# A two-block transformer kernel: x parked in DRAM around two feed-forwards, their first two jobs begun in another order, the gate's product on VectorE

## The chip, the cores and the metric

One core of one Trainium2 chip runs the whole program. The metric is the device time of one execution in microseconds (us), and of several executions the median. TensorE (PE) multiplies 128x128 blocks, VectorE (DVE), ScalarE (ACT) and GpSimd (POOL) do elementwise work, and SyncE (SP) issues most of the loads. Each engine works through its own queue in order.

## The reference

Two transformer blocks run one behind the other on 512 tokens of width 1024. All matmuls are float32. What matters here are their two feed-forwards, each on a normed x that came out of a residual addition just before:

```python
def rmsnorm(x, g):
    y = x32 * lax.rsqrt(jnp.mean(jnp.square(x32), axis=-1, keepdims=True) + EPS)
    return (y * g).astype(x.dtype)

# first block, its end
x = x + jnp.einsum('bsd,de->bse', merged, w_out[l])
h2 = rmsnorm(x, norm_mlp_g[l])
up = jnp.square(jax.nn.relu(jnp.einsum('bsd,df->bsf', h2, w_up[l])))      # 1024 -> 4096
x = x + jnp.einsum('bsf,fd->bsd', up, w_down[l])

# second block, its end
x = x + cross_attention(rms_norm(x, xattn_norm_g[l]), ...)
x = x + swiglu(rms_norm(x, ffn_norm_g[l]), w_ffn_gate[l], w_ffn_up[l], w_ffn_down[l])
return rms_norm(x, final_norm_g)

def swiglu(xn, w_gate, w_up, w_down):                                     # 1024 -> 2816
    return (jax.nn.silu(xn @ w_gate) * (xn @ w_up)) @ w_down
```

The rest (attention of three kinds, a recurrence, convolutions, gates) stands in the same program and is not touched.

## The kernel before

x lies transposed: eight tiles `x` of 128 features by 512 tokens. A float32 operand is held as two parts, hi and lo (`split_to`, L267: ACT casts hi, DVE subtracts to get lo), and a product takes three matmuls (`mm3`, L168). Every matmul is recorded on L159, so the trace tells them apart by their tiles.

**The up projections of both feed-forwards are made by a scheme with seven half-size products instead of eight.** `norm_sums` (L316) turns each pair of x tiles (one even, one odd) into operands: `ae` and `ao` (ACT, x times the gain), the sums `f1` and `f2` (DVE, L336 to L339), and then hi and lo of s1 (half of `ae`), f1, f2 and `ao`. There are four pairs. s1 needs the even tile of its pair alone; f1, f2 and `ao` need the odd one too. `weight_sums` (L347) does the same for a pair of weight slabs: raw loads on SP, casts on ACT, seven DVE operations. `halves` (L382) is one job: it makes two output tiles `ca` and `cb` out of two weight slabs by the products 1, 5, 2, 6, 7, 4, 3 (`product`, L375: twelve 128x256 matmuls each, three for each pair of x tiles). The products 1, 6, 7, 4 add up in one PSUM bank `u`, and a copy by ACT takes the bank's state after each of them (L397 to `ca`, L404 and L407 to `cb`, L411 to `ca`), so the product behind a copy waits for it. Product 5 and 3 go to `v`, product 2 to `p2`. DVE finishes with L400, L408 and L413 and hands the two tiles to `out`.

The norm's factor is not in the operands. `square` (L452) collects the squares of x on ACT and POOL (L459, L469). `rstd_tok` (L463) sums them over the features with eight small matmuls on `ones`, works out 1/sqrt on DVE (L479, then L282 to L286, thirteen small operations) and makes two diagonal tiles `dgh` and `dgl` (L491, L492). `rstd_row` (L498) spreads them over the partitions with two matmuls and a copy (L507) into `row`. Each `out` multiplies by `row` first.

**The start of a feed-forward.** The residual projection before it (`residual_stage`, L658, or `residual_keep`, L1492) takes m = 0 to 7: product into PSUM, DVE adds x (L668, L1499), then `norm_sums`. In `residual_stage` x is read back from DRAM by a POOL transfer (L666); in `residual_keep` it is in SBUF already. The first two jobs of the feed-forward start before the last pair of x is ready, with `lead=True`: they first do pairs 0 to 2 of the products 1, 5, 2, yield, then do pair 3 of them and L397 and L400, yield, then product 6 and L404, and so on. `halves_lead` (L416) lays the two jobs out in turn:

```python
for _ in range(2):
    for g in jobs:
        next(g)
r = self.rstd_tok(self.sq)
for g in jobs:
    next(g)
self.r, self.row = self.rstd_row(r)
self.sq = None
self.rounds(jobs)
```

So the norm stands between L400 and product 6 of both jobs, and `row` between products 6 and 7.

**The feed-forwards.** `ffn1` (L1011) has eight groups of two jobs; its `out` squares a relu on DVE and splits into `uh`, `ul`. `ffn2` (L1503) has five groups; jobs alternate between the gate's weights (`out_g`: times row L1525, ACT's tanh L1527, L1528, giving `tg`) and the other's (`out_u`: times row L1534, then the product of gate and up on POOL, L1535, then the split into `fah` and `fal`, L273 and L274). The down projections of a group (`downs`, L1017 and L1507) are filled in between the jobs of the next (`fill`, L438): each is twelve 128x512 matmuls into a bank and an addition into `x[m]` (L1025, L1515). x stays in SBUF all the while. `finish` (L1553) makes the last down projection and the last norm.

**What sets the order.** The text gives an order, and a planner that runs when the program is built decides each engine's queue from it: the earliest instruction of the text that it believes ready comes first, so instructions of an engine can pass each other. All elementwise tiles of 128x512 come from one pool of 56 slots (`T`, L116), and the planner hands them out in the order in which the text first writes them: of the 1186 tiles of that pool in the instruction list of the kernel before, none comes out of that order. A tile's first writer thus never stands ahead of the first writer of an earlier tile in the planner's time. The PSUM banks are eight.

Of the kernel before, what the change touches and what calls it, by code (L numbers as in the profile page):

```python
# [9 lines left out]
F32 = mybir.dt.float32  # L10
# [4 lines left out]
P = 128  # L15
S = 512
D = 1024
KT = 8
# [76 lines left out]
class Net:  # L95
# [217 lines left out]

    def norm_sums(self, x, g, kt, sq, st):  # L316


        nc = self.nc
        H = S // 2  # L320
        if kt % 2 == 0:
            a = self.T("ae")
            nc.scalar.activation(a, x, AF.Copy, scale=self.col(g, kt))
            self.square(x, sq)
            st["even"] = a
            return
        e, o = st.pop("even"), self.T("ao")
        nc.scalar.activation(o, x, AF.Copy, scale=self.col(g, kt))
        self.square(x, sq)
        kp = kt // 2  # L330
        if kp % 2 == 0:
            st["one"] = (self.R("s1h"), self.R("s1l"))
        c = (kp % 2) * H
        s1 = tuple(t[:, c : c + H] for t in st["one"])
        f1, f2 = self.T("f1"), self.T("f2")
        nc.vector.tensor_sub(f1[:, :H], e[:, H:], o[:, H:])  # L336
        nc.vector.tensor_sub(f1[:, H:], f1[:, :H], e[:, :H])
        nc.vector.tensor_sub(f2[:, :H], e[:, :H], e[:, H:])
        nc.vector.tensor_add(f2[:, H:], o[:, :H], f1[:, H:])  # L339
        self.split_to(s1[0], s1[1], e[:, :H])  # L340
        p1, p2, po = self.split(f1, s="f1"), self.split(f2, s="f2"), self.split(o, s="ao")
        cut = lambda p, i: tuple(t[:, i * H : i * H + H] for t in p)
        st.setdefault("S", []).append(
            {1: s1, 2: cut(po, 0), 4: cut(po, 1), 5: cut(p1, 0), 6: cut(p1, 1), 7: cut(p2, 0), 3: cut(p2, 1)}
        )
# [36 lines left out]
    def halves(self, wname, j, st, out, lead=False):  # L382

        nc = self.nc
        H = S // 2
        w = self.weight_sums(wname, j)
        u, v, p2 = self.PS("u"), self.PS("v"), self.PS("p2")
        if lead:
            ks = (range(KT // 2 - 1), range(KT // 2 - 1, KT // 2))
            for i, ps in ((1, u), (5, v), (2, p2)):  # L390
                self.product(ps, st, w, i, True, ks[0])
            yield
        else:
            ks = (None, range(KT // 2))
        a, b = self.T("ca"), self.T("cb")
        self.product(u, st, w, 1, True, ks[1])
        nc.scalar.copy(a[:, :H], u[:, :H])  # L397
        self.product(v, st, w, 5, True, ks[1])
        self.product(p2, st, w, 2, True, ks[1])
        nc.vector.tensor_add(a[:, :H], p2[:, :H], a[:, :H])  # L400
        if lead:
            yield
        self.product(u, st, w, 6, False)
        nc.scalar.copy(b[:, :H], u[:, :H])  # L404
        yield
        self.product(u, st, w, 7, False)
        nc.scalar.copy(b[:, H:], u[:, :H])  # L407
        nc.vector.tensor_sub(b[:, H:], v[:, :H], b[:, H:])  # L408
        yield
        self.product(u, st, w, 4, False)  # L410
        nc.scalar.copy(a[:, H:], u[:, :H])  # L411
        self.product(v, st, w, 3, False)
        nc.vector.tensor_sub(b[:, :H], v[:, :H], b[:, :H])  # L413
        out(a, b)

    def halves_lead(self, jobs):  # L416

        nc = self.nc
        for _ in range(2):
            for g in jobs:  # L420
                next(g)
        r = self.rstd_tok(self.sq)
        for g in jobs:
            next(g)
        self.r, self.row = self.rstd_row(r)
        self.sq = None
        self.rounds(jobs)

    def rounds(self, jobs):
        jobs = list(jobs)  # L430
# [227 lines left out]
    def residual_stage(self, wname, act, g, reload, halves=False):  # L658

        nc = self.nc  # L660
        sq = []
        new, nact, st = [], [], {}
        pss = self.proj_T_lead([(wname, 0), (wname, 1)], act)
        for m in range(8):
            x = self.T("x")
            nc.gpsimd.dma_start(out=x, in_=reload[m])  # L666
            ps = pss[m] if m < 2 else run(self.proj_T(wname, m, act))
            nc.vector.tensor_add(x, ps, x)  # L668
            new.append(x)
            if halves:  # L670
                self.norm_sums(x, g, m, sq, st)
            else:
                nact.append(self.norm_tile(x, g, m, sq))
        self.x, self.act, self.sq = new, st if halves else nact, sq

    def consts1(self):
        nc = self.nc
# [333 lines left out]
    def ffn1(self, g_next):  # L1011
        nc = self.nc
        st = self.act
        sq = []
        nact = []

        def downs(g, u):  # L1017
            ws = {}

            def down(m):  # L1020
                if m % 2 == 0:
                    ws[0] = self.slab("w_down", g * 4 + m // 2)
                ps = self.PS()
                self.acc_T(ps, ws[0], (m % 2) * S, u, 0, 4, True, True)
                nc.vector.tensor_add(self.x[m], ps, self.x[m])  # L1025
                if g == 7:
                    nact.append(self.norm_tile(self.x[m], g_next, m, sq))

            return [lambda m=m: down(m) for m in range(8)]

        prev = []
        for g in range(8):
            cur = []

            def out(*tiles):
                for t in tiles:
                    nc.vector.tensor_mul(t, t, self.row)
                    nc.vector.scalar_tensor_tensor(out=t, in0=t, scalar=0.0, in1=t, op0=ALU.max, op1=ALU.mult)
                    cur.append(self.split(t, s="u"))

            jobs = [self.halves("w_up", 2 * g + i, st, out, g == 0) for i in range(2)]
            if g == 0:
                self.halves_lead(jobs)
            else:
                self.fill(jobs[0], prev[:4], (1, 2))
                self.fill(jobs[1], prev[4:], (1, 2))
            prev = downs(g, cur)
        for f in prev:
            f()
        self.act, self.sq = nact, sq  # L1050
# [441 lines left out]
    def residual_keep(self, wname, act, g):  # L1492
        nc = self.nc
        sq = []
        st = {}
        pss = self.proj_T_lead([(wname, 0), (wname, 1)], act)
        for m in range(8):
            ps = pss[m] if m < 2 else run(self.proj_T(wname, m, act))
            nc.vector.tensor_add(self.x[m], ps, self.x[m])  # L1499
            self.norm_sums(self.x[m], g, m, sq, st)  # L1500
        self.act, self.sq = st, sq

    def ffn2(self):  # L1503
        nc = self.nc
        st = self.act

        def downs(g, u):  # L1507
            ws = {}

            def down(m):  # L1510
                if m % 2 == 0:
                    ws[0] = self.slab("w_fd", g * 4 + m // 2)
                ps = self.PS()
                self.acc_T(ps, ws[0], (m % 2) * S, u, 0, 4, True, True)
                nc.vector.tensor_add(self.x[m], ps, self.x[m])  # L1515

            return [lambda m=m: down(m) for m in range(8)]

        prev, gate = [], []
        for g, pairs in enumerate(((0, 1), (2, 3), (4, 5), (6, 7), (8, 9, 10))):  # L1520
            cur = []

            def out_g(*tiles):
                for z in tiles:
                    nc.vector.tensor_mul(z, z, self.row)  # L1525
                    t = self.T("tg")
                    nc.scalar.activation(t, z, AF.Tanh, scale=0.5)  # L1527
                    nc.vector.scalar_tensor_tensor(out=t, in0=t, scalar=1.0, in1=z, op0=ALU.add, op1=ALU.mult)  # L1528
                    gate.append(t)

            def out_u(*tiles):
                for z in tiles:
                    t = gate.pop(0)
                    nc.vector.tensor_mul(z, z, self.row)  # L1534
                    nc.gpsimd.tensor_mul(t, t, z)  # L1535
                    cur.append(self.split(t, 0.5, s="fa"))

            jobs = [
                self.halves(w, j, st, o, g == 0 and j == 0) for j in pairs for w, o in (("w_fg", out_g), ("w_fu", out_u))
            ]  # L1540
            if g == 0:
                self.halves_lead(jobs[:2])
                self.rounds(jobs[2:])
            else:
                n = len(prev)
                for i, job in enumerate(jobs):
                    fs = prev[i * n // len(jobs) : (i + 1) * n // len(jobs)]
                    self.fill(job, fs, (1, 1))
            prev = downs(g, cur) if g < 4 else cur
# [202 lines left out]
```

## Time and profile before

| | |
|---|---|
| median of 3 runs | 1959.29 us (1958.47 to 1959.96) |
| the profiled execution, its own time | 1957.96 us |
| its span, first to last instruction | 1956.2 us |
| granted clock of TensorE, mean | 0.982 |
| PE busy, share of the span | 1873.5 us, 96% |
| DVE busy | 1375.9 us, 70% |
| ACT, POOL busy | 868.8 us, 295.2 us |

The profile is of one execution, so its rows are added up against its own time, 1957.96 us, which is 1.33 us under the median of the runs. Busy time of PE is not PE at its peak: the clock granted to it can be half, and matmuls are then twice as long. In the rows below "<-" stands between an engine that waited and what ended its wait, or between a tile and what it is made from; names lose their numbers, so `ps` is any bank of that name.

### The profile page before, as it was taken

How to read it: one execution, taken by the hardware profiler on the slowest of the kernel's cores; microseconds unless marked ns; L12 is line 12 of the kernel's file. 1: busy time of each engine (PE TensorE's matmuls, PEld its weight loads, DVE VectorE, ACT ScalarE, POOL GpSimd, SP SyncE). 2: the span in 40 equal slices, each digit the busy share in tenths (PEclk: the TensorE clock that was granted, in tenths of full speed). 3: DMA queues.
4: the chain of work that ended last, by engine and by line, in shares of the span. 5: the costliest groups of instructions: out<-in, count | busy, mean ns of one | idle time of the engine just before them, and what ended most of it. 6: DMA issues, size and time to landing. Idle time of an engine off the chain costs nothing.

```text
span 1956.2 us, 26791 instructions
## 1 busy us (share of the span) xinstructions
PE 1873.5 (96%) x10376; PEld 1609.9 (82%) x10376; DVE 1375.9 (70%) x2548; ACT 868.8 (44%) x1499; POOL 295.2 (15%) x270
## 2 busy tenths in 40 slices
PE   8999999999979999999999999999999979999997
PEld 6787777888869999998977788888988778888886
DVE  7477777687688877867676665465566978778764
ACT  5366655454453333333343444243335544444433
POOL 2322310201210000002022110132100210110112
PEclk9999999999989999999999999999999999999998
DMA  5222322222422333334321222234422223222221
GB/s 178 81 83 92 102 72 79 88 66 65 130 86 88 107 97 98 108 97 139 96 76 65 78 85 76 98 107 135 146 97 80 87 71 108 87 87 98 86 81 60
DMA packets 54383, 183.84 MB, mean 94 GB/s; under 512 B 6528, under 2 KB 9632, under 8 KB 54256
## 3 DMA queue, kind: packets, MB, share of 16 engines
q1 hardware_dynamic: 50016, 170.78, 26.7%
q0 software_dynamic: 3552, 10.82, 1.9%
q8 instruction: 81, 1.33, 0.3%
q10 hardware_dynamic: 688, 0.53, 0.1%
q14 instruction: 46, 0.38, 0.1%
HBM read 177.87 MB, written 4.24 MB: 93 GB/s over the span
## 4 chain that ended last, share of the span: by engine, by line
PE 74%; DVE 15%; ACT 4%; DMA 3%; POOL 2%; issue 2%; DVEq 0%; SPq 0%; POOLq 0%; ACTq 0%
PE ps L159 54%; PE u L159 9%; PE v L159 3%; PE s L159 2%; PE o L159 2%; DVE wl L271 2%; PE p L159 2%; DVE wl L362 1%; DMA raw<-in_w_fg 1%; PE pv L159 1%; POOL tg L1535 1%; PE pt L163 1%; DVE sbl L367 1%; DVE sal L364 1%; DMA raw<-in_w_fu 1%
## 5 line engine op out<-in xcount | busy, mean ns | idle before, releaser
L159 PE MATMUL ps<-xx,wh 128*128 128x512 f32 x1424 | 445.6, 394 | 2.7 <-ACT wh L270 2.7
L270 ACT CAST wh<-raw 128x1024 fp32r<-128x1024 f32 (+4 forms) x252 | 255.0, 1017 | 340.0 <-PE ps L159 228.4
L271 DVE TENSOR_TENSOR wl<-raw,wh 128x1024 fp32r<-128x1024 f32 (+4 forms) x252 | 315.4, 1253 | 87.7 <-ACT wh L270 85.6
L159 PEld LDWEIGHTS ps<-xx,wh 128*128 128x128 f32 x1424 | 261.7, 188 | 59.0 <-ACT wh L270 3.1
L159 PE MATMUL ps<-xx,wl 128*128 128x512 f32 x712 | 278.0, 390 | 1.6 <-DVE wl L271 1.6
L159 PE MATMUL ps<-wh,xx 128*128 128x512 f32 (+1 forms) x512 | 157.1, 379 | 5.7 <-ACT wh L270 5.5
L159 PEld LDWEIGHTS ps<-xx,wl 128*128 128x128 f32 x712 | 133.7, 188 | 31.1 <-DVE wl L271 2.5
L159 PEld LDWEIGHTS ps<-wh,xx 128*128 128x128 f32 x512 | 95.2, 191 | 23.2 <-ACT wh L270 5.5
L459 POOL TENSOR_TENSOR sq<-sq,sq 128x512 f32<-128x512 f32 (+1 forms) x46 | 61.9, 1347 | 258.3 <-ACT sq L457 258.0
L159 PE MATMUL ps<-ul,wh 128*128 128x512 f32 x256 | 100.2, 391 | 0.0
L159 PE MATMUL ps<-uh,wh 128*128 128x512 f32 x256 | 100.0, 391 | 0.0
L159 PE MATMUL ps<-uh,wl 128*128 128x512 f32 x256 | 99.5, 389 | 0.0
L159 PE MATMUL ps<-wl,xx 128*128 128x512 f32 (+1 forms) x256 | 96.7, 378 | 2.1 <-DVE wl L271 2.1
L159 PE MATMUL ps<-fah,wh 128*128 128x512 f32 (+1 forms) x200 | 75.0, 375 | 1.4 <-ACT fah L273 1.4
L159 PE MATMUL ps<-fal,wh 128*128 128x512 f32 (+1 forms) x200 | 74.7, 373 | 0.0
L159 PE MATMUL ps<-fah,wl 128*128 128x512 f32 (+1 forms) x200 | 74.5, 372 | 0.0
L1025 DVE TENSOR_TENSOR x<-ps,x 128x512 f32<-128x512 f32 x64 | 44.1, 689 | 41.0 <-PE ps L159 41.0
L361 ACT CAST sah<-sa 128x1024 fp32r<-128x1024 f32 x38 | 39.9, 1051 | 66.3 <-DVE sa L359 62.2
L159 PE MATMUL u<-f1h,sah 128*128 128x256 f32 x152 | 46.8, 308 | 20.1 <-ACT ca L397 20.1
L1535 POOL TENSOR_TENSOR tg<-tg,ca 128x512 f32<-128x512 f32 x11 | 20.3, 1849 | 298.2 <-DVE ca L1534 298.2
L159 PE MATMUL v<-f2h,wl 128*128 128x256 f32 x304 | 60.9, 283 | 0.0
L999 POOL TENSOR_TENSOR gt<-gt,gt 128x512 f32<-128x512 f32 x24 | 36.0, 1501 | 155.4 <-DVE gt L995 155.4
(451 smaller groups left out, 5050.8 us busy)
## 6 DMA issues: line engine op xcount, KB each, us to landing
raw<-in_w_up SPq DMA_DIRECT2D x32, 512.0 KB, 3.5
raw<-in_w_down SPq DMA_DIRECT2D x32, 512.0 KB, 3.6
raw<-in_w_gate SPq DMA_DIRECT2D x24, 512.0 KB, 3.4
raw<-in_w_qkv SPq DMA_DIRECT2D x23, 512.0 KB, 3.6
raw<-in_w_fg SPq DMA_DIRECT2D x22, 512.0 KB, 3.5
raw<-in_w_fu SPq DMA_DIRECT2D x22, 512.0 KB, 3.4
raw<-in_w_fd SPq DMA_DIRECT2D x16, 512.0 KB, 3.4
raw<-in_w_conv SPq DMA_DIRECT2D x12, 512.0 KB, 3.5
```

What stands on the lines that cost most here:

```text
L159: self.nc.tensor.matmul(out, **k)
L163: self.nc.tensor.transpose(out, a, ident)
L270: nc.scalar.copy(hi, src)
L271: nc.vector.tensor_sub(lo, src, hi.bitcast(F32))
L361: nc.scalar.copy(ha, sa)
L362: nc.vector.tensor_sub(la, ra, h.bitcast(F32))
L364: nc.vector.tensor_sub(da, sa, ha.bitcast(F32))
L367: nc.vector.tensor_sub(db, sb, hb.bitcast(F32))
L459: nc.gpsimd.tensor_add(sq[0][:, sl], sq[0][:, sl], sq[1][:, sl])
L999: nc.gpsimd.tensor_add(merged[m], merged[m], t)
L1025: nc.vector.tensor_add(self.x[m], ps, self.x[m])
L1535: nc.gpsimd.tensor_mul(t, t, z)
```

## The change

1. `residual_stage` and `residual_keep` write each new x tile to a DRAM tile `xs` by a POOL transfer (`put`), and forget the SBUF tile. The first group's down projections in both feed-forwards read it back by a POOL transfer (`get`) between their matmuls and their addition.
2. In the first two jobs of a feed-forward, product 1 is written whole and copied (L397) ahead of products 5 and 2, of which pairs 0 to 2 come first; pair 3 follows after the yield, product 2 ahead of product 5. A third yield stands ahead of `out`. `halves_lead` puts the norm (`rstd_tok`) behind product 6 of both jobs, and `row` behind products 4 and 3 of the first job.
3. The product of gate and up in `out_u` moves from POOL to DVE.

```diff
+    def put(self, m, x):
+        if m == 0:
+            self.xs = self.dp.tile([8, P, S], F32, tag="xs", bufs=1, name=self.name("xs"))
+        self.nc.gpsimd.dma_start(out=self.xs[m], in_=x)
+
+    def get(self, m):
+        x = self.T("x")
+        self.nc.gpsimd.dma_start(out=x, in_=self.xs[m])
+        return x
...
         if lead:
-            ks = (range(KT // 2 - 1), range(KT // 2 - 1, KT // 2))
-            for i, ps in ((1, u), (5, v), (2, p2)):
-                self.product(ps, st, w, i, True, ks[0])
+            late = range(KT // 2 - 1, KT // 2)
+            early = range(KT // 2 - 1)
+        a, b = self.T("ca"), self.T("cb")
+        self.product(u, st, w, 1, True)
+        nc.scalar.copy(a[:, :H], u[:, :H])
+        if lead:
+            self.product(v, st, w, 5, True, early)
+            self.product(p2, st, w, 2, True, early)
             yield
+            self.product(p2, st, w, 2, True, late)
+            self.product(v, st, w, 5, True, late)
         else:
-            ks = (None, range(KT // 2))
-        a, b = self.T("ca"), self.T("cb")
-        self.product(u, st, w, 1, True, ks[1])
-        nc.scalar.copy(a[:, :H], u[:, :H])
-        self.product(v, st, w, 5, True, ks[1])
-        self.product(p2, st, w, 2, True, ks[1])
+            self.product(v, st, w, 5, True)
+            self.product(p2, st, w, 2, True)
         nc.vector.tensor_add(a[:, :H], p2[:, :H], a[:, :H])
         if lead:
             yield
...
         nc.vector.tensor_sub(b[:, :H], v[:, :H], b[:, :H])
+        if lead:
+            yield
         out(a, b)
 
     def halves_lead(self, jobs):
-        nc = self.nc
-        for _ in range(2):
-            for g in jobs:
-                next(g)
+        a, b = jobs
+        for _ in range(3):
+            next(a)
+            next(b)
         r = self.rstd_tok(self.sq)
-        for g in jobs:
+        for g in (a, b, a):
             next(g)
         self.r, self.row = self.rstd_row(r)
         self.sq = None
-        self.rounds(jobs)
+        self.rounds((a, b))
...
             if halves:
+                self.put(m, x)
                 self.norm_sums(x, g, m, sq, st)
...
                 self.acc_T(ps, ws[0], (m % 2) * S, u, 0, 4, True, True)
+                if g == 0:
+                    self.x[m] = self.get(m)
                 nc.vector.tensor_add(self.x[m], ps, self.x[m])
...
                     t = gate.pop(0)
                     nc.vector.tensor_mul(z, z, self.row)
-                    nc.gpsimd.tensor_mul(t, t, z)
+                    nc.vector.tensor_mul(t, t, z)
                     cur.append(self.split(t, 0.5, s="fa"))
```

`put` and `get` stand in the same way in `residual_keep` (behind L1499) and in both `downs` (L1025, L1515).

## Rows read from the trace of the kernel before

**Rows 1.** The page's busy time by engine.

```profile
PE 1873.5 (96%) x10376; PEld 1609.9 (82%) x10376; DVE 1375.9 (70%) x2548; ACT 868.8 (44%) x1499; POOL 295.2 (15%) x270
```

**Rows 2.** Stretches: length, busy PE, PEld, DVE, ACT, POOL, PE clock, DMA share.

```profile
552.00:593.00 41.00, 30.26 (x183) 28.29 (x182) 29.33 (x58) 18.77 (x34) 6.19 (x6) 0.79 0.20 64
593.00:885.00 292.00, 292.00 (x1840) 265.01 (x1839) 225.34 (x320) 111.08 (x165) 0.00 (x0) 1.00 0.33 102
884.00:920.00 36.00, 36.00 (x163) 29.74 (x162) 26.19 (x30) 16.52 (x24) 14.06 (x15) 1.00 0.43 145
1544.00:1584.00 40.00, 29.67 (x184) 28.13 (x183) 29.07 (x58) 17.34 (x29) 6.08 (x2) 0.79 0.15 53
1584.00:1910.00 326.00, 304.18 (x2083) 280.93 (x2081) 252.34 (x346) 136.37 (x217) 41.86 (x22) 0.98 0.27 91
```

**Rows 3.** PE in time, first lead, 569 to 593: start, duration, [idle before].

```profile
569.06 1.87 PE L159 MATMUL ps<-ones,sq 128*128 128x2 f32 x8 [2.48 <-POOL sq L469]
...
578.04 0.28 PE L159 MATMUL u<-f1h,sal 128*128 128x256 f32 x1
581.91 0.51 PE L159 MATMUL ps<-dgh,onesr 128*128 128x512 f32 x1 [3.59 <-DVE dgh L491]
...
582.76 0.28 PE L159 MATMUL u<-f2h,sbh 128*128 128x256 f32 x1
...
587.13 0.28 PE L159 MATMUL u<-aoh,sbh 128*128 128x256 f32 x1
...
592.77 0.28 PE L159 MATMUL v<-f2h,wl 128*128 128x256 f32 x1
```

**Rows 4.** ACT in time, first lead: the first copies to cb.

```profile
581.30 0.64 ACT L404 COPY cb<-u 128x256 f32<-128x256 f32 x2
```

**Rows 5.** DVE in time, first lead: `dgh`, then the first and last of `out`.

```profile
580.46 0.47 DVE L491 TENSOR_SCALAR dgh<-ident,s 128x128 fp32r<-128x128 f32 x2
...
589.17 0.69 DVE L1037 TENSOR_TENSOR ca<-ca,row 128x512 f32<-128x512 f32 x1 [1.01 <-ACT ca L411]
...
599.46 0.69 DVE L271 TENSOR_TENSOR ul<-cb,uh 128x512 fp32r<-128x512 f32 x1
```

**Rows 6.** Two of PE's waits in the second lead, 1544 to 1584: total, times, longest.

```profile
PE u L159 <- ACT cb L404: 3.4, 1, 3.4
PE ps L159 <- DVE dgh L491: 2.7, 1, 2.7
```

**Rows 7.** PE in time, second lead: where product 6 starts and the jobs end.

```profile
1556.28 0.58 PE L159 MATMUL v<-f1l,sah 128*128 128x256 f32 x1 [0.51 <-DVE f1l L271]
...
1561.44 0.56 PE L159 MATMUL u<-f1h,sah 128*128 128x256 f32 x1
...
1583.85 0.28 PE L159 MATMUL v<-f2h,wl 128*128 128x256 f32 x1
```

**Rows 8.** PE's waits in the second feed-forward, 1584 to 1912.

```profile
PE u L159 <- ACT ca L397: 20.1, 12, 2.4
PE ps L159 <- ACT fah L273: 1.4, 1, 1.4
```

**Rows 9.** The gated product on POOL, second tile of a job: ns min/median/max, first and last start.

```profile
L1535 POOL TENSOR_TENSOR tg<-tg,cb x11: 1267/2126/2276, 1589.7 to 1908.0; 128x512 f32<-128x512 f32 x11
```

**Rows 10.** DVE in time, second feed-forward: two subtractions of one size.

```profile
1742.72 1.99 DVE L362 TENSOR_TENSOR wl<-raw,wh 128x1024 fp32r<-128x1024 f32 x1
...
1745.83 1.21 DVE L367 TENSOR_TENSOR sbl<-sb,sbh 128x1024 fp32r<-128x1024 f32 x1
```

**Rows 11.** A 10 us stretch behind one of the longer waits, columns as in rows 2.

```profile
1750.00:1760.00 10.00, 10.00 (x57) 8.93 (x56) 5.53 (x10) 2.41 (x5) 0.00 (x0) 0.83 0.15 52
```

**Rows 12.** Transfers between x and DRAM on POOL, and their time to landing.

```profile
L1067 POOL DMA_DIRECT2D xd<-x x8: 539/557/562, 892.6 to 911.9; - x8
L666 POOL DMA_DIRECT2D x<-xd x8: 536/553/553, 1344.2 to 1378.7; - x8
...
DMA to landing us min/median/max: 2.3/2.8/5.2
```

More of the change, by code (lines that the diff above doesn't have):

```diff
@@ L673, in residual_stage @@
                 nact.append(self.norm_tile(x, g, m, sq))
-        self.x, self.act, self.sq = new, st if halves else nact, sq
+        self.x, self.act, self.sq = [None] * 8 if halves else new, st if halves else nact, sq
     def consts1(self):
@@ L1499, in residual_keep @@
             nc.vector.tensor_add(self.x[m], ps, self.x[m])
+            self.put(m, self.x[m])
             self.norm_sums(self.x[m], g, m, sq, st)
+        self.x = [None] * 8
         self.act, self.sq = st, sq
@@ L1514, in down @@
                 self.acc_T(ps, ws[0], (m % 2) * S, u, 0, 4, True, True)
+                if g == 0:
+                    self.x[m] = self.get(m)
                 nc.vector.tensor_add(self.x[m], ps, self.x[m])
```

## The prediction

> **What bounds the kernel now.** I read the page first. PE is busy for 1873.5 of 1956.2 us [rows 1], so the kernel is a chain of matmuls, and a change that leaves their number alone can win only where PE stands idle or runs at half its clock. Next I read the busy time by stretches. The first feed-forward behind its start keeps PE busy for all of 292 us at full clock: nothing to gain there. Its start (552 to 593) has 30.3 us of work in 41, the second start (1544 to 1584) 29.7 in 40, both at a mean granted clock of 0.79, and the second feed-forward 304.2 in 326 at 0.98 [rows 2]. These three places hold 10.7, 10.3 and 21.8 us of idle time, 42.8 in all, and some time at half clock on top. The change touches just these three. So the question is what ends PE's waits there, and for that I read the waits of PE in each.
>
> In the first start the longest wait is 3.6 us, for `dgh`, the norm's diagonal tile [rows 3]. The reader should see what stands in the way: product 6 of both jobs ends at 578.04, product 7 needs ACT's copies of it to `cb` (L404), and those come at 581.30 [rows 4], just after DVE has begun `dgh` at 580.46 [rows 5]. `cb` is first written behind the norm in the text, and slots go out in the text's order, so the copies were planned behind the norm's DVE chain. In the second start the same two things cost 3.4 us (`cb`) and 2.7 us (`dgh`) [rows 6]. In the second feed-forward nearly all waits are one line: product 6 for `ca` (L397), 20.1 us in 12 waits, and one for `fah`, 1.4 us [rows 8]. `ca` of a job is first written behind `fah` of the job before, and ACT's queue has it behind `fah`, which waits for the product on POOL. That one lasts 1.27 us at its shortest and 2.13 at the median [rows 9]: POOL and DVE hold each other up, and a DVE subtraction of 1.21 us takes 1.99 beside it [rows 10].
>
> **The parts of the change.**
>
> *The norm later.* It removes nothing; it moves the eight `ones` matmuls, the DVE chain, `dgh`, `dgl` and the two `row` matmuls behind product 6, and so puts `cb`'s first write ahead of `dgh`'s. Behind product 6 PE then has products 7, 7, 4 and 3 without the norm. The 48 matmuls of products 4 and 3 start from 587.13 to 592.77 [rows 3], 0.12 us apart, so the four products are 48 x 0.12 = 5.8 us of cover for the norm's chain.
>
> First start: from product 6's end (578.2) to the end of the two jobs (592.9) it is 14.7 us. The 72 matmuls are 72 x 0.12 = 8.6 us, the two `row` matmuls 0.85 (581.91 to 582.76) [rows 3]: 9.5 us. The difference, 5.2 us, is the wait of 3.6 and about 1.5 of half clock behind it (product 7 of both jobs, 24 matmuls, took 582.76 to 587.13, 4.4 us instead of 2.9). Next late is `out`: its DVE chain runs 11 us, 589.17 to 600.1 [rows 5], and the first down projection needs its last piece. It starts as soon as the first job's product 3 is done, 5.8 us behind product 6, at about 584.2, and ends at about 595, 5 us earlier. I take 4.5. Below, -2, if the chain runs later than its cover and PE's queue has `row` ahead of the second job's product 4; above, 5.2 plus the 2.5 us that PE waits for the last square ahead of `ones` [rows 3], 7.7. The `ones` matmuls (1.87 us, in a gap today) may cost up to their length where no gap is left; that is inside these bounds.
>
> Second start: product 6 has its operands at 1556.28 and starts at 1561.44; the jobs end at 1583.97 [rows 7]. From 1556.28 that is 27.7 us: 6.1 of the two waits [rows 6], 2.7 of norm matmuls by the first start's rows, and 109 matmuls (13 left of pair 3, 24 of product 6, 72 behind them), which are 13.1 us at full clock; the other 5.8 us are half clock. The waits go; of the half clock I give back half, as the work behind the wait for `f1h` stays slow at first: 6.1 + 2.9 = 9.0, less 1.5 for ACT's copies standing behind weight casts in its queue. I take 7.5; below 2.7 (only `dgh`), above 11.9.
>
> *Product 1 whole and first, product 2 ahead of 5.* The planner already takes what is ready; pair 3 of product 1 needs only the even tile. Six matmuls of 0.12 us come sooner at best, 0.7 us; at worst a copy stands in ACT's queue ahead of a cast, as long. I take 0, covered by DVE's operands, which are what PE waits for then.
>
> *The gated product on DVE.* It removes 22 POOL instructions and adds 22 on DVE at 0.69 us (the price of L1037 [rows 5]): 15 us of DVE, which is busy 252 of 326 us there [rows 2], and it takes off the holding up, 0.8 us for each [rows 10], 17 us. So DVE's load stays; the gain is the chain: 2.13 + about 0.2 to the next engine becomes 0.69, 1.6 us less for each of ten waits of up to 2.4 us, and for `fah` at the end. Of the 21.5 us of waits I count 20 to jobs that end in `out_u` (those that end in `out_g` have no POOL in them, and wait little); cutting each by 1.6 takes 15; a quarter I give back for a weight operation of 1.2 us that the planner may put between the new product and its neighbours on DVE. That leaves 13. Some of the longer waits are followed by half clock (0.83 for 10 us, so 3.4 us at half speed and 1.7 lost [rows 11]; four such stretches, 6.8 in all); shorter waits should spare most: 5. I take 18; below 4, above 27, all of it.
>
> *x through DRAM.* 16 transfers out and 16 back, all on POOL's queue. The nearest row for the way out is the same transfer at the end of the first feed-forward: 0.56 us of POOL each between the same squares, landing in 2.3 to 5.2 us [rows 12], with PE busy for all 36 us [rows 2]. It lies beside the squares, whose sum is wanted later than before: 0. If that cover were gone, the last would delay `ones` by 0.56. The way back: the transfer's slot follows `cb`'s in the text, so it starts about when the down projection does and lands 2.8 us later; the addition waits that long on DVE, a bank is held longer, and DVE's next job waits behind it. I take 1 us for each feed-forward, 2 in all; below a cost of 0, above 16 x (2.8 + 0.56) = 54, each fully exposed. Freed slots are worth nothing that I can see: no wait of PE in rows 3, 6 or 8 is for a free slot.
>
> Here the Trainium skill speaks against the change (SBUF — State Buffer, SBUF: two separate sides): transfers issued from GpSimd need it to write descriptors, and VectorE can lock it out, so that about 620 ns become about 3100. By that, as an estimate, 32 x 2.5 = 80 us would be added if all of it lay on the path. The trace does not show it: the issues stay at 0.54 to 0.56 us with DVE 73% busy [rows 2, 12].
>
> **The sum.** 4.5 + 7.5 + 0 + 18 - 2 = 28 us less than the profiled execution's 1957.96, which gives 1930; the median of the runs stands 1.33 above that execution, so 1931. About 0.2% (4 us) is what a measurement of this kernel can tell from no change.
>
> **The rivals.**
>
> *The starts keep their length* (14%). The norm's chain on DVE stands among weight operations; if it takes longer than its 5.8 us of cover, PE's queue waits at `row` as it does now at `dgh`. For it: `dgh` began only at 580.46, 9.5 us behind the end of `ones` [rows 3, 5]. Against it: DVE was then held by work that waited for product 6. Time: 1931 + 12 = 1943. It is also the case where the new order says nothing new to the planner.
>
> *VectorE takes the product's gain back* (12%): the new operation queues behind weight operations. Of 18 us, 6 are left: 1943. For it, DVE is 77% busy there; against it, the first feed-forward has the same load and no wait at all [rows 2].
>
> *All of it* (8%): the three places lose three quarters of their idle time and the half clock behind it, 45 us: 1914.
>
> *The way back is exposed* (5%). Each of the 16 additions holds DVE's queue until its transfer lands, and the next job's weights are late behind it. At 54 us it is 1931 + 54 - 2 = 1983, slower. It decides from 1.9 us of exposed time for each transfer. For it: landing takes up to 5.2 us [rows 12]. Against it: the addition is wanted only when its bank is.
>
> *No change* (4%): the waits go to the next late thing, the weights' loads.
>
> **The numbers.** The forecast, 1931, has 57%; its own range is 1922 to 1940. With the two rivals at 1943 the range is 1918 to 1946; outside it lie the slow case, no change and most of the large gain. Faster 57 + 14 + 12 + 8 = 91%, the same 4%, slower 5%.
>
> **What would show it.** Right: no wait of PE for `dgh` or `cb` in either start, and L404 ahead of L491; PE's waits for `ca` in the second feed-forward at 6 us or less, no L1535 on POOL, its DVE price 0.69, and L362 at 1.2 us throughout; POOL issues of 0.56. Wrong: a wait for `row`'s matmul at products 4, `ca` still at 15 us or more, DVE idle for the transfers back in the first group, or PE idle in 593 to 640.

## The result and the profile after

| | before | after |
|---|---|---|
| median of 4 runs each | 1958.88 us (1955.32 to 1959.96) | 1924.92 us (1922.52 to 1927.55) |
| ratio | | 0.983, 95% interval 0.9812 to 0.9849 |
| the profiled execution, its own time | 1957.96 us | 1925.78 us |
| its span | 1956.2 us | 1924.0 us |

The median of before has one run more in it than the 1959.29 us of the table above. The change makes the kernel 34 us faster; the forecast was 1931, its range 1918 to 1946. By the size it looks like a sum that came out a little small. It is more than that: one term of it overlooked a queue, and two others made up for it.

The line numbers of after lie higher by 6 to 22: L403 is the copy to `ca` behind product 1 (it was L397), L417 and L420 the copies to `cb`, L506 `dgh`, L683 the residual's addition, L474 and L484 the squares on POOL, L681 the read-back of x from DRAM in `residual_stage`, L1557 the gated product; L319 is `put`, L323 `get`. First the page's busy time by engine, against [rows 1].

```profile
PE 1868.6 (97%) x10376; PEld 1604.5 (83%) x10376; DVE 1371.2 (71%) x2570; ACT 868.4 (45%) x1499; POOL 271.1 (14%) x280
```

As many matmuls as before, and nearly as much busy time. So the 32 us of span came out of idle time and half clock, as they had to. To see where, I cut both spans at five places where the same matmul starts: the first one of the residual projection (`mgh`), the first of the third job of the first feed-forward (`s1h`, behind the two leading jobs), the first of the second feed-forward, the first of its third job, and the first matmul of the last norm (`dg`). The rows of before, from the view of single tiles (ns min/median/max, first and last start) and from PE in time (start, duration):

```profile
L159 PE MATMUL ps<-mgh,wh x128: 389/389/389, 509.0 to 1384.8; 128*128 128x512 f32 x128
...
592.89 0.28 PE L159 MATMUL u<-s1h,wh 128*128 128x256 f32 x1
...
1544.79 0.28 PE L159 MATMUL u<-s1h,wh 128*128 128x256 f32 x1
...
1583.97 0.28 PE L159 MATMUL u<-s1h,wh 128*128 128x256 f32 x1
...
L159 PE MATMUL ps<-dg,ones x4: 377/506/793, 1938.7 to 1947.5; 128*128 128x256 f32 x4
```

The same of after:

```profile
L159 PE MATMUL ps<-mgh,wh x128: 389/389/390, 510.7 to 1384.4; 128*128 128x512 f32 x128
...
592.56 0.28 PE L159 MATMUL u<-s1h,wh 128*128 128x256 f32 x1
...
1544.38 0.28 PE L159 MATMUL u<-s1h,wh 128*128 128x256 f32 x1
...
1574.60 0.28 PE L159 MATMUL u<-s1h,wh 128*128 128x256 f32 x1
...
L159 PE MATMUL ps<-dg,ones x4: 377/506/792, 1904.3 to 1913.1; 128*128 128x256 f32 x4
```

The differences of these starts, with the first stretch and the last one up to the span's end, give a ledger in us:

| stretch | before | after | difference | forecast |
|---|---|---|---|---|
| up to the residual's first matmul | 509.0 | 510.7 | +1.7 | 0 |
| residual and first start | 83.9 | 81.9 | -2.0 | -4.5 |
| first feed-forward and all up to the second | 951.9 | 951.8 | -0.1 | +1 |
| second start | 39.2 | 30.2 | -9.0 | -7.5 |
| second feed-forward, up to the last norm | 354.7 | 329.7 | -25.0 | -18 + 1 |
| last norm to the end | 17.5 | 19.7 | +2.2 | 0 |

The +1.7 is no part of the change: nothing is changed ahead of 509, and over the kernels below that stretch lasts from 508.6 to 511.0 us (in e12, which has a wait of its own there, 512.6). The rest needs the waits. PE's waits of after in the second feed-forward, 1576 to the end (total, times, longest), against [rows 8]:

```profile
PE ps L159 <- DVE dg L501: 3.7, 1, 3.7
PE u L159 <- ACT ca L403: 1.3, 1, 1.3
```

The 20.1 us of waits for `ca` are 1.3. In 1690 to 1890 the mean granted clock rose from 0.97 to 1.00 with them, and PE is busy 198.5 of 200 us there instead of 187.1. In the second start (1530 to 1576) one wait for the norm is left, 1.4 us, and none for `cb`, against [rows 6]:

```profile
PE ps L159 <- DVE dgh L506: 1.4, 1, 1.4
PE u L159 <- ACT s1h L270: 1.2, 1, 1.2
PE p L159 <- ACT aoh L270: 1.1, 1, 1.1
PE u L159 <- DVE s1l L271: 0.7, 1, 0.7
```

In the first start (540 to 602) the waits for the norm are gone too, but two others grew, so that the whole gained little. `s1h` had cost 1.1 there and `sq` 2.5:

```profile
PE ps L159 <- POOL sq L484: 3.7, 1, 3.7
PE u L159 <- ACT s1h L270: 3.4, 2, 3.1
PE u L159 <- DVE s1l L271: 2.1, 2, 1.2
```

The 3.7 us for `sq` belong to the last pair of x, the 3.1 us for `s1h` to the pair before it: ACT casts that `s1h` behind `ao` of the same pair, and `ao` waited for its x. DVE's addition and ACT's two steps, in after:

```profile
557.93 0.69 DVE L683 TENSOR_TENSOR x<-ps,x 128x512 f32<-128x512 f32 x1 [2.75 <-DMA x<-in_xT]
...
558.66 0.72 ACT L338 ACTIVATE ao<-x,cols 128x512 f32<-128x512 f32 x1 [2.77 <-DVE x L683]
...
559.81 0.39 ACT L270 CAST s1h<-ae 128x256 fp32r<-128x256 f32 x1
```

So x came late. DVE's waits of after (520 to 575) say what made it so:

```profile
DVE x L683 <- PE ps L159: 6.5, 1, 6.5
DVE x L683 <- DMA x<-in_xT: 6.4, 3, 2.8
```

The second of these lines has no counterpart before. The additions of the residual wait 6.4 us for x read back from DRAM. POOL in time shows why; two of its read-backs of this stage, with what stands ahead of them, in after:

```profile
553.22 0.54 POOL L319 DMA_DIRECT2D xs<-x  x1 [8.12 <-DVE x L683]
553.75 0.54 POOL L681 DMA_DIRECT2D x<-in_xT  x1
...
567.10 0.54 POOL L319 DMA_DIRECT2D xs<-x  x1 [4.97 <-DVE x L683]
567.63 0.54 POOL L681 DMA_DIRECT2D x<-in_xT  x1
```

The reader should see the order in the queue: `put` (L319) waits 8.12 us for DVE's addition, and the read-back of the next x (L681), which shows no wait of its own, stands behind it and leaves at 553.75; it is the one for which the addition above waits until 557.93. The last read-back stands in the same way behind 4.97 us. Before, POOL issued the read-backs in pairs, behind its squares: the tile that after reads at 553.75 was in the pair that left from 542.14, and the last pair left from 556.26. The chain closes on itself: addition, put, read-back, next addition.

### The profile page after: what moved, and what is told of

The parts are those of the page before. It is cut to its first block, busy times and chain, and to the rows that moved or that the text cites. A ratio compares the mean times of both kernels' runs of the same rounds, so it can differ in the third digit from the quotient of the medians.

```text
span 1924.0 us, 26869 instructions
## 1 busy us (share of the span) xinstructions
PE 1868.6 (97%) x10376; PEld 1604.5 (83%) x10376; DVE 1371.2 (71%) x2570; ACT 868.4 (45%) x1499; POOL 271.1 (14%) x280
## 4 chain that ended last, share of the span: by engine, by line
PE 79%; DVE 11%; ACT 3%; issue 3%; DMA 2%; POOL 2%; SPq 0%; DVEq 0%; POOLq 0%; ACTq 0%
PE ps L159 56%; PE u L159 10%; PE v L159 5%; PE p L159 2%; PE s L159 2%; PE o L159 2%; DVE wl L271 1%; PE pv L159 1%; DMA raw<-in_w_fg 1%; PE pt L163 1%; DMA x<-in_xT 1%; ACT wh L270 1%; DMA raw<-in_w_fd 1%; DVE wl L372 1%; ACT L L823 0%
## 5 line engine op out<-in xcount | busy, mean ns | idle before, releaser
L474 POOL TENSOR_TENSOR sq<-sq,sq 128x512 f32<-128x512 f32 (+1 forms) x46 | 62.2, 1353 | 317.8 <-ACT sq L472 317.4
L159 PEld LDWEIGHTS ps<-wl,xx 128*128 128x128 f32 x256 | 49.3, 193 | 9.8 <-DVE wl L271 2.0
L159 PEld LDWEIGHTS ps<-uh,wl 128*128 128x128 f32 x256 | 48.1, 188 | 10.2
```

Source lines behind the costliest of these rows:

```text
L159: self.nc.tensor.matmul(out, **k)
L474: nc.gpsimd.tensor_add(sq[0][:, sl], sq[0][:, sl], sq[1][:, sl])
```

## The experiments

All ratios below are to the kernel before, whose medians in the three sets of runs were 1959.08 (e1 to e4), 1958.02 (e5 to e8) and 1959.54 us (e9 to e12). After's ratio is that of the first table.

### Each part alone, and two of the three

`e1_no_park` is after without `put` and `get`:

```diff
-                self.put(m, x)
...
-                if g == 0:
-                    self.x[m] = self.get(m)
```

> Parts 2 and 3 without part 1: x stays in SBUF. Theory A, the puts hold up the first start: POOL issues each put behind DVE's addition, and the read-back of the next x from DRAM stands behind it in POOL's queue; DVE then waits 2.75 and 1.02 us for those read-backs. Without puts the first start gives its whole 4.5 us instead of 2.0, and nothing else moves: about 1922, 2.5 under the changed kernel, and no wait of DVE for x read from DRAM. Rival B, the 8 freed slots are what let the second feed-forward gain 25 instead of 18: without parking it is about 1932. Rival C, parking does nothing at all: 1925.

`e2_gate_only` is before with one line changed:

```diff
-                    nc.gpsimd.tensor_mul(t, t, z)
+                    nc.vector.tensor_mul(t, t, z)
```

> Part 3 alone. The prediction's sum gives -18, so 1941. Theory A, the second feed-forward's 25 us between its first start and the last norm all belong to the gated product (about 18.5 of waits and 6.5 of half clock): 1934, PE's wait for the copy to ca under 3 us. Rival, VectorE takes the product's gain back without the later start: -6, 1953.

`e3_starts_only` is before with the whole of part 2, `halves` and `halves_lead` of after:

```diff
-        for _ in range(2):
-            for g in jobs:
-                next(g)
+        for _ in range(3):
+            next(a)
+            next(b)
         r = self.rstd_tok(self.sq)
-        for g in jobs:
+        for g in (a, b, a):
             next(g)
...
```

> Part 2 alone, x in SBUF, the product on POOL. Theory A, the two starts do not depend on the other parts, and without puts the first gives 4.5: -4.5 - 9 = 1945. The prediction's sum: -4.5 - 7.5 = 1947. Rival, the starts' gain is given back in the second feed-forward's waits for ca, which stay: 1950 to 1955.

`e4_park_only` is before with `put` and `get` and nothing else:

```diff
+                self.put(m, x)
...
+                if g == 0:
+                    self.x[m] = self.get(m)
```

> Part 1 alone. The prediction: +2, 1961. Theory A, the puts delay the read-backs of the first residual on POOL's queue and nothing hides that: the first start longer by 2.5 to 5, so 1961 to 1964, and no wait of PE in the first group for a transfer back. Rival B, the freed slots help by themselves: 1952 or less.

Measured, each with its ledger of the profiled run in us:

| | us | ratio, 95% interval | first start | second start | second feed-forward | end |
|---|---|---|---|---|---|---|
| before | | | 83.9 | 39.2 | 354.7 | 17.5 |
| after | 1924.92 | 0.983 (0.9812 to 0.9849) | 81.9 | 30.2 | 329.7 | 19.7 |
| e1, parts 2 and 3 | 1918.67 | 0.9787 (0.9774 to 0.98) | 78.4 | 29.9 | 328.9 | 17.5 |
| e2, part 3 | 1933.78 | 0.9868 (0.9854 to 0.9881) | 83.7 | 39.2 | 330.1 | 17.5 |
| e3, part 2 | 1943.35 | 0.9914 (0.9901 to 0.9928) | 78.4 | 30.0 | 353.1 | 17.5 |
| e4, part 1 | 1963.65 | 1.0025 (1.0015 to 1.0036) | 87.4 | 40.8 | 356.4 | 19.7 |

What follows. The product on VectorE is worth 25.3 us (1959.08 - 1933.78), the starts 15.7, and the two together 40.4, so they add up. Parking x costs 4.6 us alone (the profiled run of e4, 1968.13 us, lies 4.5 above its median, so its columns add up to 9.0 more than those of before) and 6.2 on top of the others (1924.92 - 1918.67). It is a loss, and the change is faster in spite of it. The rival by which the eight freed slots help falls: e4 is slower, and e1, which keeps x in its slots, is the faster one. Theory A had the direction right in e1 and the size too small (1922): it had only the first start's 2.5 us, and 3.5 are lost there, 2.2 at the end, and about 1 us in the two other stretches. The 2.2 us at the end occur in the two parked kernels and in none of the others of this table. e4's time came out as its theory A had it, and e2's (1934) too, though e2's wait for `ca` is 3.5 us and not under 3; e3 is 1.6 us below its theory A. In e2 PE's waits for `ca` in the second feed-forward fell as in after:

```profile
PE u L159 <- ACT ca L397: 3.5, 5, 1.1
```

### The norm's place or the order of the products

`e5_late_norm_old_order` is e1 with the old order in `halves`:

```diff
-        self.product(u, st, w, 1, True)
-        nc.scalar.copy(a[:, :H], u[:, :H])
...
+            for i, ps in ((1, u), (5, v), (2, p2)):
+                self.product(ps, st, w, i, True, ks[0])
```

> Parts 2 and 3 without part 1 (1918.7), but with the products 1, 5, 2 of the two leading jobs in the old order; the norm stays late. The prediction: the order of the products is worth nothing, the norm's place all of it: 1918 to 1920. Rival: the early copy of product 1 and product 2 ahead of 5 carry half of the starts' 14.7 us: about 1926.

`e6_early_norm_new_order` is e1 with the old `halves_lead`:

```diff
-        for _ in range(3):
-            next(a)
-            next(b)
+        for _ in range(2):
+            for g in jobs:
+                next(g)
         r = self.rstd_tok(self.sq)
```

> The other half of the same cut: the new order of the products 1, 5, 2, but the norm back between the addition behind product 2 and product 6, and no third stop ahead of out. The prediction: the starts' gain is lost whole, 1933 to 1934 (the product on VectorE alone gave 1933.8), with waits of PE for dgh of 3 us in both starts and for cb in the second. Rival: half of it stays, about 1926.

Measured: e5 1917.68 us (0.9791, 0.9778 to 0.9805), with 78.1 and 30.1 us for the two starts; e6 1931.09 us (0.9861, 0.9848 to 0.9875), with 84.0 and 37.9. e5 and e1 can't be told apart. So the norm's place carries the gain of the starts, and the order of the products adds nothing to it. In e6 the old waits are back; PE in its two starts:

```profile
PE ps L159 <- DVE dgh L504: 3.6, 1, 3.6
...
PE u L159 <- ACT cb L417: 4.3, 1, 4.3
PE ps L159 <- DVE dgh L504: 2.2, 1, 2.2
```

e6's median is 2.7 us under e2's, but the two stand in different sets, and their intervals overlap, so it is not shown that the new order is worth something with an early norm; the second start of e6's profiled run is 1.3 us shorter.

### What parking costs, and where

`e7_park_on_sp` is after with the other queue in `put` and `get`:

```diff
-        self.nc.gpsimd.dma_start(out=self.xs[m], in_=x)
+        self.nc.sync.dma_start(out=self.xs[m], in_=x)
...
-        self.nc.gpsimd.dma_start(out=x, in_=self.xs[m])
+        self.nc.sync.dma_start(out=x, in_=self.xs[m])
```

> The changed kernel with the transfers of x out and back on SP's queue in place of POOL's. Theory A: parking costs 6.2 us (1924.9 against 1918.7) because the puts hold up the read-backs on POOL's queue (3.4 in the first start) and because 32 more transfers from POOL lengthen the end of the program by 2.2; on SP's queue both go, and the time is 1919 to 1920, the first start 78.4 us from the first residual matmul, as without parking. Rival: on SP's queue the puts wait for the additions ahead of the weight loads, so that these are late: 1930 or more. Rival: it is the moving of the bytes that costs, wherever it is issued: 1925.

`e8_puts_only` is after with `put` but without `get`:

```diff
-                if g == 0:
-                    self.x[m] = self.get(m)
```

> The changed kernel with the puts on POOL but without the way back: x stays in SBUF too, and nothing reads the copies in DRAM. Theory A: the puts alone cost the 3.4 us in the first start; the second start and the second feed-forward are those without parking (1.1 us less); of the 2.2 us at the end of the program half goes with half of the transfers: 1922 to 1923. Rival: the way back is what costs, in slots and in DVE waiting: 1919.

Measured: e7 2047.95 us (1.0456, 1.0439 to 1.0473), e8 1922.27 us (0.9808, 0.9791 to 0.9825). e7 is the first rival, far beyond the price that it had been given (1930): the same 32 transfers on the other queue cost 123 us more than on POOL. Its SP queue in time, in the first residual:

```profile
580.05 0.38 SPq L149 DMA_DIRECT2D raw<-in_w_out  x1
595.22 0.32 SPq L319 DMA_DIRECT2D xs<-x  x1
595.63 0.38 SPq L149 DMA_DIRECT2D raw<-in_w_out  x1
609.56 0.32 SPq L319 DMA_DIRECT2D xs<-x  x1
609.97 15.59 SPq L362 DMA_DIRECT2D raw<-in_w_up  x6
```

One weight slab for each put, and the put waits for the addition, which waits for the matmuls, which wait for the slab ahead: 14 to 16 us a round, where the 24 matmuls of one product of the residual, 0.227 us apart in the trace, take 5.4. PE's waits of the whole e7 name the weights:

```profile
PE ps L159 <- ACT wh L270: 82.9, 14, 7.0
```

e8 came out as its theory A had it, and splits the 6.2 us. Its first start takes 81.6 us and DVE waits 5.9 us there for x read from DRAM, so the 3.2 us lost there belong to the puts, and its last stretch takes 18.4. The gets would be the other 2.7 us by the medians (1924.92 - 1922.27), but that is not clear of noise: e8's runs lie between 1917.28 and 1924.15, those of after between 1922.52 and 1927.55. By the two profiled runs the gets cost 1.3 at the end (19.7 - 18.4) and about 1.0 from the second start to the last norm.

### Whether it is the read-backs behind the puts

`e10_reload_first` is after with the eight read-backs ahead of the loop in `residual_stage`:

```diff
+        xs = [self.T("x") for _ in range(8)]
+        for m in range(8):
+            nc.gpsimd.dma_start(out=xs[m], in_=reload[m])
         pss = self.proj_T_lead([(wname, 0), (wname, 1)], act)
         for m in range(8):
-            x = self.T("x")
-            nc.gpsimd.dma_start(out=x, in_=reload[m])
+            x = xs[m]
```

> The changed kernel (1924.9) with all eight read-backs of x in the two residual stages issued on POOL ahead of the loop, so that no put stands ahead of one. Theory A, the puts' 3.4 us in the first start are the read-backs held up in POOL's queue: the first start takes 78.4 us instead of 81.9 and the whole 1921.5 or less; DVE has no wait there for x read from DRAM. Rival, the puts cost by their own transfers or by holding up the squares on POOL: the first start stays at 81 to 82 us, 1924 to 1925.

`e11_no_park_reload_first` is e5 with the same edit:

> The late norm with the old order of products and the product on VectorE, x in SBUF (1917.7), with the read-backs ahead of the loop on POOL as well. Theory A: there the last additions of the residual stand at 562.1 and 565.7, behind read-backs that POOL issued only at 556.3 and 557.3; issued earlier, the additions can come some us sooner, the first start shortens by 2 to 4: 1914 to 1916. Rival: DVE is busy without a gap until 562.8 with the weights' sums, so the additions come no sooner: 1917.7. Rival: the eight slots taken early are missing elsewhere: 1920 or more.

`e12_no_park_reload_first_sp` is e11 with `nc.sync` in place of `nc.gpsimd` in that edit:

> As the one before, with these 16 read-backs on SP's queue ahead of the residual's weights. Theory A, by the end of the program: it was 2.2 us longer with 32 more transfers on POOL, 0.9 with 16, and none with 32 on SP, so 16 fewer on POOL take about 1 us off the time from the last norm matmul to the end (17.5 to 16.5): 1 us below the one before. Rival: a read-back that waits for a slot on SP's queue makes the weights behind it late, as the puts did on SP: 1925 to 1960.

Measured: e10 1915.81 us (0.9777, 0.9764 to 0.9791), e11 **1911.47 us** (0.9757, 0.9744 to 0.9771), e12 1926.57 us (0.9832, 0.9818 to 0.9845). In e10 POOL issues the eight reads in one go, and the last put stands alone:

```profile
512.98 4.27 POOL L680 DMA_DIRECT2D x<-in_xT  x8
...
560.78 0.56 POOL L319 DMA_DIRECT2D xs<-x  x1
```

DVE has no wait for x left in that stage. The first start fell to 72.1 us, not to 78.4: the edit takes away what the puts cost (3.5) and 6.3 us more. e11 shows the like of these without parking: 72.4 us against e5's 78.1. And with the reads first, the first start is as long with the puts (e10) as without (e11, which has the old order of the products, worth nothing in e5): the puts themselves cost nothing there, only what stood behind them. e11's last two additions stand at

```profile
552.77 0.68 DVE L682 TENSOR_TENSOR x<-ps,x 128x512 f32<-128x512 f32 x1
558.31 0.68 DVE L682 TENSOR_TENSOR x<-ps,x 128x512 f32<-128x512 f32 x1
```

and those of before at

```profile
562.08 0.68 DVE L668 TENSOR_TENSOR x<-ps,x 128x512 f32<-128x512 f32 x1
565.65 0.68 DVE L668 TENSOR_TENSOR x<-ps,x 128x512 f32<-128x512 f32 x1
```

Both moved up by 7 to 9 us, although DVE did not wait for x before. DVE's queue had the additions behind weight operations; with the reads issued early they stand ahead of them. That the planner's due times for the reads did this is what I take it to be; the runs show only the new order. e11 beats before by 48 us and after by 13. It is the kernel to keep: the late norm, the product on VectorE, the reads first, x in SBUF.

e12's 1926.57 lies in the rival's range, but no read waits for a slot on SP in the first residual: the eight leave in 3.8 us from 482.55, and the weights behind them from 486.49, where e11 has 484.46. Two us later on the queue became more on PE, by a way that is not followed here. PE waits 3.7 us for a cast of weights just ahead of its first residual matmul, which comes at 512.6 where e11 has it at 509.3. The first start behind it takes 75.3 us, 2.9 more than in e11, and its first 17.4 us have a mean granted clock of 0.84 where e11 has 1.00. The stretch between the starts grew from 951.9 to 957.6, with another wait of 3.8 for a cast of weights. The theory that it was to test failed too: with 16 transfers fewer on POOL the end took 17.5 us as before, no less; the last section says why.

### Whether POOL and VectorE hold each other up

`e9_pool_beside` is e1 with a multiplication on POOL that nobody needs:

```diff
                     nc.vector.tensor_mul(t, t, z)
+                    nc.gpsimd.tensor_mul(self.T("idle"), z, z)
```

> Parts 2 and 3 without part 1 (1918.7), and beside each of the 22 gated products on VectorE a multiplication of the same size on POOL that squares z into a tile which nobody reads; its result is no part of the output. Theory A, the gain of part 3 is the shorter chain from the row's product to fah: POOL's work stands in no chain, so the time stays within 3 us, 1918 to 1921, though DVE's subtractions of 1.2 us beside it stretch to 2 as they did before. Rival, half of the gain is that POOL and VectorE no longer hold each other up: 1925 to 1931, and PE waits for ca again.

Measured: 1929.56 us (0.985, 0.9837 to 0.9864), 10.9 above e1, and the rival's. From the second start to the last norm it takes 371.0 us where e1 takes 358.8, and PE waits for `ca` again, 5.0 us where e1 has 1.6, and 2.8 for `fal`:

```profile
PE u L159 <- ACT ca L403: 5.0, 5, 1.5
```

DVE in time there:

```profile
1726.24 1.42 DVE L1550 TENSOR_TENSOR tg<-tg,ca 128x512 f32<-128x512 f32 x1
1729.31 1.52 DVE L274 SCALAR_TENSOR_TENSOR fal<-tg,fah 128x512 fp32r<-128x512 f32 x1
1730.76 0.68 DVE L1550 TENSOR_TENSOR tg<-tg,cb 128x512 f32<-128x512 f32 x1
```

And POOL in the same stretch:

```profile
1726.07 1.04 POOL L1551 TENSOR_TENSOR idle<-ca 128x512 f32<-128x512 f32 x1 [28.66 <-DVE ca L1549]
1728.40 1.89 POOL L1551 TENSOR_TENSOR idle<-cb 128x512 f32<-128x512 f32 x1 [1.29 <-DVE cb L1549]
```

The product that starts 0.17 us behind POOL's takes 1.42 us instead of 0.68, the subtraction of `fal` beside POOL's second 1.52 and that one 1.89; the next product, with POOL idle, 0.68 again. No long weight operation was hit much (L372 at most 1.73 us); the work of the chain itself was, since POOL's operand came free at the same moment. The Trainium skill (SBUF — State Buffer, SBUF: two separate sides) states that the two engines share one pair of ports which one of them holds for its whole instruction while the other is blocked, for VectorE operations with two operands in SBUF against a POOL operation that reads it. These rows agree with that in the main: POOL's first operation had 0.87 us left when DVE's began, and that one took 0.74 longer. Over the whole kernel DVE's busy time rose with the 22 operations from 1372.4 to 1387.4 us, 15.0, for the same work of its own. The run tells what the sharing costs when it falls on the chain, not how much of the 25 us it is: the extra tile also takes a slot of the pool 22 times and holds `z` longer, and the run does not separate that.

## Why the prediction was right or wrong

**What bounds the kernel.** Right: PE's busy time stayed, and the three places that it named are the three that moved. The first feed-forward behind its start keeps PE busy for all of 593 to 885 in both.

**The norm later, first start (-4.5).** The mechanism was right, the copies to `cb` come ahead of `dgh` in both starts (L417 at 582.11 and 584.37, `dgh` at 585.81 in the first), and the term measures 5.5 in e3 and e1 (83.9 to 78.4), inside its bounds. That is the 5.2 of wait and half clock which the prediction had found; that `out` would hold it to 4.5 did not occur. The ledger shows only 2.0 because the puts took 3.5 back.

**The norm later, second start (-7.5).** 9.2 in e3. The cover of four products was too short by 1.4 us: between `ones` and `dgh` the small steps stand among weight operations of 1.2 us, as the first rival had said; so its sign "no wait of PE for `dgh`" failed in this start. In after, PE's waits of the whole start fell by 5.4 us (3.6, 3.4, 2.7 and 0.5 against 1.4, 1.2, 1.1, 0.7 and 0.4); the other 3.6 of its 9.0 are half clock, of which I had counted 2.9.

**Product order (0).** Right where it was asked, e5 against e1.

**The gated product (-18).** The step that failed in size: 25.3 in e2, close to the upper bound, 27. The sum itself does not come out: 15 less a quarter is 11, not the 13 that it took, so by its own steps the term was 16. The "about 0.2 to the next engine" in it stood in no row; in the trace of before ACT's cast to `fah` starts 0.03 us behind POOL's product. The quarter that it gave back "for a weight operation of 1.2 us" did not occur, and the waits of 21.5 us went to 3.5 in e2 and 1.3 in after instead of 8.5. The 5 us of half clock came out as 6 (24.6 of the stretch in e2, less 18.4 of waits), nearly all that [rows 11] and its three likes held. The rival "VectorE takes the product's gain back" falls. The price of 0.69 held, and so did the reason why DVE could take the work: its busy time went from 1375.9 us to 1373.2 in e2 with 22 operations more, so some 18 us of holding up went, where the prediction had 17. In after the product is always 0.68 to 0.69, and L372, which is [rows 10]'s L362, lies between 1.21 and 1.22 us in the second feed-forward. The following line is of after, single line, ns min/median/max.

```profile
L1557 DVE TENSOR_TENSOR tg<-tg,cb x11: 683/685/694, 1581.5 to 1874.6; 128x512 f32<-128x512 f32 x11
```

**x through DRAM (+2).** The step that failed in kind. The 0 for the 16 transfers out, "beside the squares", looked at what a put lasts (0.56 us) and at the squares behind it. It did not ask what a put waits for, nor what else is on POOL's queue: in `residual_stage` the read-backs of x, which [rows 12] list (L666) for the later stage with the same line. 3.2 to 3.5 us went there. The end of the program, 2.2 us, was in no term. The gets, for which I had the 2, cost about 1 us in the feed-forwards, a size that the runs do not hold clear of noise. The sum, 6.2, was inside the bounds of 0 and 54, and the rival "the way back is exposed" falls: DVE does not wait for a get. What the Trainium skill sets against the change (SBUF — State Buffer, SBUF: two separate sides: a transfer from GpSimd of about 620 ns that takes about 3100 beside a copy on VectorE) no run here shows; all that VectorE ran beside the puts were TENSOR_TENSOR operations, not copies. The 16 puts and 16 gets of after, views of single lines, ns min/median/max:

```profile
L319 POOL DMA_DIRECT2D xs<-x x16: 544/557/562, 522.1 to 1551.2; - x16
...
L323 POOL DMA_DIRECT2D x<-xs x16: 536/536/558, 574.2 to 1633.0; - x16
```

**The sum.** -28 forecast, -34 measured, -12 and -18 and +2 against -15.7, -25.3 and about +6. Two terms were too small by 3.7 and 7.3 us and one by about 4 the other way, so that the total came as near as 6 us is in part luck. Freed slots were worth nothing, as said.

## What to carry to other kernels

Before a transfer that has to wait is put on a queue, list what stands behind it there and waits for nothing: the loads in the same loop are the price, not the transfer's half microsecond, and a queue that carries weights was by far the worst place for it here. Issue loads without a dependency ahead of the loop, on a queue where nothing urgent stands behind them. Where a chain of small steps crosses from one engine to another and back, the same step on the busier engine can be the shorter way, if that takes the second engine's hold on the first one off the chain.

## What was not expected of the hardware

The end of the program, behind the last store's issue, was longer in the kernels with more transfers from POOL. From the last `dg` matmul to the end it is 8.7 us before and in e1, e2, e3, e5, e6, e9 and e11 to 0.1; 10.9 in after, e4 and e10 with 32 more transfers on POOL; 9.5 in e8 with 16 more; 8.6 in e7, whose 32 are on SP. But with 16 fewer than before, e12, it is 8.6 too. The timeline does not list what runs there, but the view of the kernel's last line does: behind its last operation POOL has a DRAIN, the longest of three (ns min/median/max). In e12, before, e8 and after, whose POOL issues 38, 54, 70 and 86 transfers:

```profile
L1761 POOLq DRAIN  x3: 46/98/5047, 1915.0 to 1922.2; - x3
...
L1747 POOLq DRAIN  x3: 46/93/6352, 1948.6 to 1955.9; - x3
...
L1764 POOLq DRAIN  x3: 46/93/7662, 1912.4 to 1920.6; - x3
...
L1769 POOLq DRAIN  x3: 46/98/8969, 1914.2 to 1923.7; - x3
```

Each 16 transfers add 1.31 us to it, 0.08 us for each, and in e7 it is 6.36 us as before. With 54 transfers or fewer it ends ahead of SP's own closing instructions (in before at 1954.95, and those at 1955.34), so that it costs nothing; with 70 and 86 it ends behind them, 2.2 us in after, and the end comes 0.8 us behind it in each of the four kernels that have so many. That is why 16 more cost 0.9 us, 32 more 2.2, and 16 fewer gave nothing. What the DRAIN does for each transfer no run shows.
